# A two-dimensional prefix-sum diagonal: one scan pair for all row groups, another head piece, a finer last load

## The chip, the cores and the metric

The kernel runs on one core of one Trainium2 chip. The metric is device time in microseconds (us) of that core. "The time" is the median of several executions; "the span" is the part of one profiled execution that the hardware profiler covers. All start times below are counted from the start of that span. Engines are named as the profile names them: PE (TensorE), DVE (VectorE), ACT (ScalarE), POOL (GpSimd) and SP (SyncE).

## The reference

The input is four float32 matrices of 4224 x 4224. For each, the two-dimensional prefix sum is taken, its diagonal is read, and the diagonal is summed up once more:

```python
ps = np.cumsum(np.cumsum(x, axis=1), axis=2)
diag = np.diagonal(ps, axis1=1, axis2=2)
return np.cumsum(diag, axis=1).astype(np.float32)
```

Entry i of the diagonal is the sum of the square of rows 0..i and columns 0..i. So it grows, from i-1 to i, by d[i]: the elements of column i above the diagonal, plus the elements of row i up to and with the diagonal. The output is d summed up twice along i. Every element of x is used once, 285.47 MB are read, and only 4 x 4224 numbers are written.

## The kernel before, in words

**Groups.** The rows of one matrix are cut into NG = 11 groups of GW = 384 rows. A group is loaded as one "strip": 128 partitions with 3 neighbouring rows each, all 4224 columns, cast from float32 to bf16 by the transfer. POOL's queue issues these loads (`load_group`, L64). Six strip buffers rotate (NBUF), so a load is issued when the strip six places earlier has been used up.

**What is made of a strip.** For group g the columns fall into three kinds. Columns right of the group lie above the diagonal: PE adds them down over the rows (`columns`, one matmul of 384 columns for each row plane q and each later group j). The selector, a bf16 matrix of zeros with one column of ones, puts the sum into row j of the accumulator d[11, 384] in PSUM. In the group's own 384 columns, `masked` on DVE (L187) multiplies with an upper-triangle mask: the product `mu` goes to PE as the part above the diagonal, and its row sum `ru` is kept. Left of that, whole rows are summed: ACT takes some 9/16 of the columns (`act_sum`, L178), DVE the rest and the group's own columns (`rs`, L297). Row sums minus `ru` give the part at and below the diagonal.

**The end of a matrix.** `sum_up` (L268, L269) forms `rows`; three float32 matmuls with an identity turn them into d. DVE runs two scans over d[11, 384] from zero (L207, L215), PE turns the ends of the groups into the carries of later groups (`carry_ps`, with the small matrices `earlier` and `apart`), and `between` adds `step * carry1 + carry2` to the second scan: the "y step" (L228, L236), on DVE for the first three matrices, on POOL for the last. SP writes y out (L237).

**The last matrix** is arranged so that little is left after the last byte. Its last group (384 rows) is not loaded as a strip. A float32 `head` (the last 128 rows, last 1056 columns) is loaded on SP's queue at the very start. `diag_a`, the 256 x 384 diagonal piece of the other rows, is loaded between strips 0 and 1 of the last matrix and worked on after strip 1. What is left comes behind strip 9: 256 rows in two column pieces (`acuts`), then the last 128 rows in three (`tcuts`). Group 10 has an accumulator of its own, `d_last`, and its own pair of scans `lc`, seeded with `lcarry`. What the late pieces add is summed over rows (`arows` for the 256 rows, `ttot` for the 128) by three helpers at once: PE adds column blocks onto each other with an identity (`fold_in`), ACT sums a second share, DVE a third. Float32 matmuls against weight matrices (`fin_a`, `fin_b`) turn these row sums into what they add to the output, and two adds on DVE (`yl`, L409) and two stores on SP (L410) finish.

The order of the instructions on each engine is written out by hand (`manual_schedule`): an engine runs its instructions in program order.

Of the kernel before, what the change touches and what calls it, by code (L numbers as in the profile page):

```python
# [17 lines left out]
def kernel(  # L18
# [8 lines left out]

    nc = tc.nc

    B, H, W = x.shape  # L30
    N = H
# [4 lines left out]
    LB = B - 1  # L36
    NBUF = 6
# [17 lines left out]
    TB = N - P  # L55
    T0 = N - GW
    HEAD = 1056
    head = last.tile([P, HEAD], FP32, name="head")
    nc.sync.dma_start(out=head, in_=x[LB, TB:N, N - HEAD : N])

# [10 lines left out]

    sel = consts.tile([P, 2 * NG - 1], BF16, name="sel")
    nc.vector.memset(sel, 0.0)
    nc.vector.memset(sel[:, NG - 1 : NG], 1.0)
    ones_col = sel[:, NG - 1 : NG]

    def selector(j):
        return sel[:, NG - 1 - j : 2 * NG - 1 - j]

    def upper_masks(f, w):  # L80
        ums = []
        for q in range(f):
            um = consts.tile([P, w], BF16, name=f"um_{f}_{q}")
            nc.vector.memset(um, 1.0)
            nc.gpsimd.affine_select(  # L85
                out=um,
                in_=um,
                compare_op=ALU.is_gt,
                fill=0.0,
                base=-q,  # L90
                pattern=[[1, w]],
                channel_multiplier=-f,
            )
            ums.append(um)
        return ums

    um3 = upper_masks(F, GW)
# [14 lines left out]
    step_i = consts.tile([NG, GW], I32, name="step_i")  # L112
    nc.gpsimd.iota(step_i, pattern=[[1, GW]], base=1, channel_multiplier=0)
    step = consts.tile([NG, GW], FP32, name="step")
    nc.gpsimd.tensor_copy(out=step, in_=step_i)
# [3 lines left out]
    nc.vector.memset(earlier, 1.0)  # L119
    nc.gpsimd.affine_select(  # L120
        out=earlier,
        in_=earlier,
        compare_op=ALU.is_gt,
        fill=0.0,
        base=0,
        pattern=[[1, NG]],
        channel_multiplier=-1,
    )
    apart_i = consts.tile([NG, NG], I32, name="apart_i")
    nc.gpsimd.iota(apart_i, pattern=[[GW, NG]], base=-GW, channel_multiplier=-GW)  # L130
    apart = consts.tile([NG, NG], FP32, name="apart")
    nc.gpsimd.tensor_copy(out=apart, in_=apart_i)
    nc.gpsimd.affine_select(
        out=apart,
        in_=apart,
        compare_op=ALU.is_gt,
        fill=0.0,
        base=0,
        pattern=[[1, NG]],
        channel_multiplier=-1,  # L140
    )
    um2 = upper_masks(2, GW)
    um1 = upper_masks(1, P)[0]

    def weights(name, q, f, w):

        wi = consts.tile([P, w], I32, name=name + "_i")
        nc.gpsimd.iota(wi, pattern=[[1, w]], base=1 - q, channel_multiplier=-f)
        wt = consts.tile([P, w], FP32, name=name)
        nc.gpsimd.tensor_copy(out=wt, in_=wi)  # L150
        nc.gpsimd.affine_select(
            out=wt,
            in_=wt,
            compare_op=ALU.is_ge,
            fill=0.0,
            base=-q,
            pattern=[[1, w]],
            channel_multiplier=-f,
        )
        return wt  # L160

    w2 = [weights(f"w2_{q}", q, 2, GW) for q in range(2)]
    w1 = weights("w1", 0, 1, P)

# [8 lines left out]
    DUMP = 2176  # L173

    def act_sum(acc, src):
        w = src.shape[-1]
        dump = dumpool.tile([P, DUMP], BF16, name="dump")
        nc.scalar.activation(  # L178
            out=dump[:, :w], in_=src, func=ACT.Copy, accum_out=acc
        )  # L180

    def scalar_cols(g):

        return 0 if g == 0 else (g * GW) * 9 // 16 // 32 * 32
# [11 lines left out]


    NT = 6
    tsum = last.tile([P, NT], FP32, name="tsum")
    hsum = last.tile([P, 2], FP32, name="hsum")  # L200
    hmu = last.tile([P, P], BF16, name="hmu")
    nc.vector.reduce_sum(out=hsum[:, 0:1], in_=head, axis=AX.X)
    masked(hmu, head[:, HEAD - P : HEAD], um1, hsum[:, 1:2])
    nc.vector.tensor_sub(out=tsum[:, 0:1], in0=hsum[:, 0:1], in1=hsum[:, 1:2])

    def scans(d, rows, width, init1, init2, c12):
        nc.vector.tensor_tensor_scan(  # L207
            out=c12[:rows, 0, :width],
            data0=ones_row[:rows, :width],
            data1=d,  # L210
            initial=init1,
            op0=ALU.mult,
            op1=ALU.add,
        )
        nc.vector.tensor_tensor_scan(  # L215
            out=c12[:rows, 1, :width],
            data0=ones_row[:rows, :width],
            data1=c12[:rows, 0, :width],
            initial=init2,
            op0=ALU.mult,  # L220
            op1=ALU.add,
        )

    def between(b, ng, c12, carry_ps, eng):
        carry = smalls.tile([NG, 2], FP32, name="carry")
        nc.vector.tensor_copy(out=carry[:ng, :], in_=carry_ps[:ng, 0:2])  # L226
        y = smalls.tile([NG, GW], FP32, name="y")
        eng.tensor_scalar(  # L228
            out=y[:ng, :],
            in0=step[:ng, :],  # L230
            scalar1=carry[:ng, 0:1],
            scalar2=carry[:ng, 1:2],
            op0=ALU.mult,
            op1=ALU.add,
        )
        eng.tensor_add(out=y[:ng, :], in0=y[:ng, :], in1=c12[:ng, 1, :])  # L236
        nc.sync.dma_start(  # L237
            out=out[b, : ng * GW].rearrange("(g i) -> g i", i=GW), in_=y[:ng, :]
        )

    for b in range(B):
        whole = b < LB
        ng = NG if whole else NG - 1
        d = psum_d.tile([NG, GW], FP32, name="d")
        d_last = None
        if not whole:
            d_last = psum_s.tile([1, GW], FP32, name="d_last")

        first = {"d": True, "l": True}

        def columns(j, lo, hi, rhs):

            if j < ng:
                matmul(d[:, lo:hi], selector(j), rhs, start=first["d"])
                first["d"] = False
            else:
                matmul(d_last[:, lo:hi], ones_col, rhs, start=first["l"])
                first["l"] = False
# [5 lines left out]
        nc.vector.memset(sa[:, 0, :], 0.0)  # L264

        def sum_up(g0, g1):
            gs = slice(g0, g1)
            nc.vector.tensor_add(out=rows[:, gs], in0=rs[:, gs], in1=sa[:, gs])  # L268
            nc.vector.tensor_sub(out=rows[:, gs], in0=rows[:, gs], in1=ru[:, gs])  # L269

        def fold_in(o, src, c0, c1, w):

            for c in range(c0, c1, w):
                matmul(o, ident_h, src[..., c : c + w], start=c == c0)

        for g in range(ng):
            lo, hi = g * GW, (g + 1) * GW
            strip = prefetched.pop((b, g), None)
# [5 lines left out]
            ws = scalar_cols(g)  # L284
            wp = 0
            if not whole and g == ng - 1:

                wp, ws = 1280, 1280 + 1536
                fold9 = psum_s.tile([P, F, 160], FP32, name="fold")
                fold_in(fold9, strip, 0, wp, 160)  # L290
            for q in range(F):
                mu = mup.tile([P, GW], BF16, name="mu")
                masked(mu, strip[:, q, lo:hi], um3[q], ru[:, g, q : q + 1])
                columns(g, 0, GW, mu)
                if ws > 0:
                    act_sum(sa[:, g, q : q + 1], strip[:, q, wp:ws])
            nc.vector.reduce_sum(  # L297
                out=rs[:, g, :], in_=strip[:, :, ws:hi], axis=AX.X
            )
            if not whole and g == 0:  # L300

                diag_a = last.tile([P, 2, GW], BF16, name="diag_a")
                src_a = x[b, T0:TB, :].rearrange("(p f) w -> p f w", f=2)
                nc.gpsimd.dma_start(out=diag_a, in_=src_a[:, :, T0:N])
            if not whole and g == 1:
                NA = 6
                asum = last.tile([P, 2, NA], FP32, name="asum")
                asub = last.tile([P, 2, 2], FP32, name="asub")
                nc.vector.reduce_sum(out=asub[:, :, 0], in_=diag_a, axis=AX.X)
                for q in range(2):  # L310
                    mu = mup.tile([P, GW], BF16, name="mu")
                    masked(mu, diag_a[:, q, :], um2[q], asub[:, q, 1:2])
                    columns(NG - 1, 0, GW, mu)
                columns(NG - 1, GW - P, GW, hmu)
                nc.vector.tensor_sub(
                    out=asum[:, :, 0], in0=asub[:, :, 0], in1=asub[:, :, 1]
                )

        if whole:
            sum_up(0, ng)  # L320
        else:

            strip = strips.tile([P, F, N], BF16, name="strip")
            acuts = [(1536, T0), (0, 1536)]
            for c0, c1 in acuts:
                nc.gpsimd.dma_start(out=strip[:, :2, c0:c1], in_=src_a[:, :, c0:c1])  # L326
# [10 lines left out]
        for q in range(F):  # L337
            matmul(d[:ng, q : GW : F], rows[:, :ng, q], ident)
# [104 lines left out]
```

## Time and profile before

| what | value |
|---|---|
| time, median of 7 runs (lowest to highest) | 671.68 us (671.22 to 673.96) |
| the profiled execution's own time | 671.23 us |
| its span, and what lies around it | 669.5 us, 1.73 us |
| busy PE / DVE / ACT / POOL | 228.3 / 255.9 / 152.9 / 36.5 us |
| software DMA queue | 7440 packets, 142.47 MB written, 99.4% of 16 engines' span |
| mean granted PE clock | 0.648 |

The strips' transfers fill the span; the engines work in bursts of 3 to 8 us after each landing and idle between. Two stretches are not covered by the stream of strips: the first few us, and the work behind the last landings.

### The profile page before, as it was taken

The page shows a single profiled execution, that of the slowest core. Times are in us where ns is not written, and L with a number is a line of the kernel's source. Part 1 is how long each engine was busy: PE and PEld are TensorE (multiplying, and loading weights), DVE is VectorE, ACT ScalarE, POOL GpSimd, SP SyncE. Part 2 cuts the span into 40 slices and gives each one's busy share as a digit, 9 for nine tenths or more (in the row PEclk, how much of TensorE's full clock was granted, in tenths as well). Part 3 has the DMA queues.
Part 4 walks back from the last instruction along what each step waited for, and adds up shares of the span by engine and source line. Part 5 has one row for each costly group of instructions (what it writes and reads, how often), then busy time and mean ns, then how long its engine had stood idle before and what let it go on. Part 6 is the DMA issues. An engine that isn't in the chain of part 4 may idle for free.

```text
span 669.5 us, 2644 instructions
## 1 busy us (share of the span) xinstructions
PE 228.3 (34%) x865; PEld 96.6 (14%) x865; DVE 255.9 (38%) x370; ACT 152.9 (23%) x247; POOL 36.5 (5%) x77
## 2 busy tenths in 40 slices
PE   0454532211155543221125443322213453332225
PEld 0221211000022211100012221110001221111102
DVE  2122333344623333334472222333456222233457
ACT  0011222233301112223330111222342011122344
POOL 6000000000000000000000000000000000000000
PEclk9877676655577776655557676665555676766657
DMA  8999999999999999999999999999999999999995
GB/s 202 218 218 219 218 219 218 217 218 219 218 219 214 215 214 214 217 217 217 219 218 219 218 217 218 217 217 217 218 217 216 217 218 216 215 218 217 218 207 116
DMA packets 7686, 143.23 MB, mean 214 GB/s; under 512 B 845, under 2 KB 1402, under 8 KB 2170
## 3 DMA queue, kind: packets, MB, share of 16 engines
q0 software_dynamic: 7440, 142.47, 99.4%
q1 hardware_dynamic: 234, 0.61, 0.3%
q8 instruction: 6, 0.10, 0.1%
q14 instruction: 6, 0.05, 0.0%
HBM read 285.47 MB, written 0.07 MB: 426 GB/s over the span
## 4 chain that ended last, share of the span: by engine, by line
another core or an unknown queue 53%; DVE 35%; DMA 7%; PE 3%; issue 1%; POOL 0%; DVEq 0%; POOLq 0%
DVE rs L297 23%; DVE mu L187 9%; DMA strip<-in_x_dram 7%; PE d L169 3%; DVE c L215 1%; DVE c L207 1%; PE fin_a L169 0%; DVE lc L215 0%; POOL strip L64 0%; DVE y L236 0%; PE carry_ps L169 0%; PE fin_b L169 0%; DVE lc L207 0%; DVE rows L269 0%
## 5 line engine op out<-in xcount | busy, mean ns | idle before, releaser
L169 PE MATMUL d<-strip,sel 128*11 128x384 bf16 x630 | 174.8, 457 | 354.9 <-DMA strip<-in_x_dram 354.9
L178 ACT ACTIVATE dump<-strip 128x640 bf16<-128x640 bf16 (+12 forms) x123 | 140.2, 1140 | 510.1 <-DMA strip<-in_x_dram 507.6
L187 DVE SCALAR_TENSOR_TENSOR mu<-strip,um 128x384 bf16<-128x384 bf16 x129 | 65.2, 555 | 394.8 <-DMA strip<-in_x_dram 394.8
L297 DVE TENSOR_REDUCE rs<-strip 128x3 f32<-128x1152 bf16 (+11 forms) x43 | 167.1, 3886 | 0.0
L169 PEld LDWEIGHTS <-sel 128*11 128x11 bf16 (+1 forms) x792 | 90.1, 114 | 527.8 <-issue 505.7
L64 POOL DMA_DIRECT2D strip<-in_x_dram x43 | 23.0, 537 | 534.7 <-PE d L169 281.6
L169 PE MATMUL d<-mu,sel 128*11 128x384 bf16 x129 | 37.4, 399 | 40.5 <-DVE mu L187 40.5
L178 ACT ACTIVATION_READ_ACCUMULATOR dump<-strip 128x1 f32 x123 | 22.9, 186 | 0.0
L169 PE MATMUL d_last<-strip,sel 128*1 128x384 bf16 x30 | 9.0, 424 | 11.9 <-DMA strip<-in_x_dram 11.9
L169 PE MATMUL d<-ident,rows 128*11 128x128 f32 (+1 forms) x24 | 5.2, 379 | 21.4 <-DVE rows L269 21.4
L187 DVE DVE_READ_ACCUMULATOR mu<-strip,um 128x1 f32 x129 | 10.7, 83 | 0.0
L169 PEld LDWEIGHTS d<-ident,rows 128*11 128x11 f32 (+1 forms) x24 | 2.5, 118 | 25.4 <-DVE rows L269 16.9
L207 DVE TENSOR_TENSOR_SCAN c<-ones_row,d 11x384 f32<-11x384 f32 (+1 forms) x4 | 3.8, 942 | 4.8 <-PE d L169 4.7
L169 PE MATMUL fold<-strip,ident_h 128*128 128x480 bf16 (+1 forms) x13 | 4.5, 524 | 1.5 <-DMA strip<-in_x_dram 1.5
L215 DVE TENSOR_TENSOR_SCAN c<-ones_row,c 11x384 f32<-11x384 f32 (+1 forms) x4 | 3.8, 945 | 0.1
L228 POOL TENSOR_SCALAR y<-step,carry 10x384 f32<-10x384 f32 x1 | 0.7, 651 | 54.2 <-DVE carry L226 54.2
L169 PE MATMUL carry_ps<-c,earlier 11*11 11x2 f32 (+2 forms) x10 | 0.8, 159 | 7.7 <-DVE c L215 7.7
L330 POOL DMA_DIRECT2D strip<-in_x_dram x3 | 1.6, 537 | 22.1 <-PE d L169 14.2
L169 PEld LDWEIGHTS <-ident_h 128*128 128x128 bf16 x19 | 2.1, 124 | 4.7 <-issue 4.1
L85 POOL TENSOR_SCALAR_AFFINE_SELECT um<-um 128x384 bf16<-128x384 bf16 (+1 forms) x6 | 2.7, 480 | 0.1
L326 POOL DMA_DIRECT2D strip<-in_x_dram x2 | 1.4, 709 | 13.4 <-PE d L169 13.4
L169 PE MATMUL fin_a<-w,arows 128*1 128x256 f32 x4 | 2.1, 634 | 0.0
(64 smaller groups left out, 37.5 us busy)
## 6 DMA issues: line engine op xcount, KB each, us to landing
strip<-in_x_dram POOLq DMA_DIRECT2D x43, 3168.0 KB, 82.9
strip<-in_x_dram POOLq DMA_DIRECT2D x1, 1152.0 KB, 74.7
strip<-in_x_dram POOLq DMA_DIRECT2D x1, 768.0 KB, 77.6
strip<-in_x_dram POOLq DMA_DIRECT2D x1, 568.0 KB, 65.5
head<-in_x_dram SPq DMA_DIRECT2D x1, 528.0 KB, 3.6
diag_a<-in_x_dram POOLq DMA_DIRECT2D x1, 192.0 KB, 84.0
strip<-in_x_dram POOLq DMA_DIRECT2D x1, 160.0 KB, 65.8
strip<-in_x_dram POOLq DMA_DIRECT2D x1, 64.0 KB, 57.6
```

The source lines that it names most:

```text
L64: nc.gpsimd.dma_start(out=t, in_=x[b, r0 : r0 + GW, :].rearrange("(p f) w -> p f w", f=F))
L85: nc.gpsimd.affine_select(out=um, in_=um, compare_op=ALU.is_gt, fill=0.0, base=-q, pattern=[[1, w]], channel_multiplier=-f,)
L169: nc.tensor.matmul(o, lhsT=lhsT, rhs=rhs, start=start, stop=False, skip_group_check=True)
L178: nc.scalar.activation(out=dump[:, :w], in_=src, func=ACT.Copy, accum_out=acc)
L187: nc.vector.scalar_tensor_tensor(out=o, in0=i, scalar=1.0, in1=m, op0=ALU.mult, op1=ALU.mult, accum_out=acc,)
L207: nc.vector.tensor_tensor_scan(out=c12[:rows, 0, :width], data0=ones_row[:rows, :width], data1=d, initial=init1, op0=ALU.mult, op1=ALU.add,)
L215: nc.vector.tensor_tensor_scan(out=c12[:rows, 1, :width], data0=ones_row[:rows, :width], data1=c12[:rows, 0, :width], initial=init2, op0=A ...
L228: eng.tensor_scalar(out=y[:ng, :], in0=step[:ng, :], scalar1=carry[:ng, 0:1], scalar2=carry[:ng, 1:2], op0=ALU.mult, op1=ALU.add,)
L297: nc.vector.reduce_sum(out=rs[:, g, :], in_=strip[:, :, ws:hi], axis=AX.X)
L326: nc.gpsimd.dma_start(out=strip[:, :2, c0:c1], in_=src_a[:, :, c0:c1])
L330: nc.gpsimd.dma_start(out=tail[:, 0, c0:c1], in_=x[b, TB:N, c0:c1])
```

## The change

- **One accumulator and one scan pair for all 11 groups.** Row k = (j + 1) mod 11 of d holds group j, so that group 10 is row 0 and the ten others are rows 1 to 10. `d_last`, `lc`, `lcarry` and the scans for them go.
- **Scans seeded by weighted totals.** DVE first sums each row of d (`pu` column 0), and sums d times 384, 383, ..., 1 (`to_end`; `pu` column 1). PE makes the carries of these sums, and the scans start from the carries. The y step goes; SP writes the second scan out, in two stores for a whole matrix.
- **The head piece** is now the 256 rows' last 528 columns (rows h * 128 + p instead of 2p + h), masked once for each half at the start. The piece of the last 128 rows that comes between the strips, `diag_b`, is 128 x 128.
- **The late pieces.** The 256 rows come in columns 1536 to 3696 and 0 to 1536; the last 128 rows in four pieces of 1664, 1408, 704 and 320 columns.
- The row sums of strip 9 of the last matrix go through `parts` and one reduction over it; the sums of strips 0 to 8 are formed before strip 9 is worked on.

```diff
-    head = last.tile([P, HEAD], FP32, name="head")
-    nc.sync.dma_start(out=head, in_=x[LB, TB:N, N - HEAD : N])
+    HC = 528
+    src_a = x[LB, T0:TB, :].rearrange("(h p) w -> p h w", p=P)
+    head = last.tile([P, 2, HC], FP32, name="head")
+    nc.sync.dma_start(out=head, in_=src_a[:, :, N - HC : N])
...
+    def row_of(j):
+        return (j + 1) % NG
...
+    to_end = counted("to_end", NG, GW, [(0, GW, GW, -1, 0)])
...
             if not whole and g == 0:
-                diag_a = last.tile([P, 2, GW], BF16, name="diag_a")
-                nc.gpsimd.dma_start(out=diag_a, in_=src_a[:, :, T0:N])
+                diag_b = last.tile([P, P], BF16, name="diag_b")
+                nc.gpsimd.dma_start(out=diag_b, in_=x[b, TB:N, TB:N])
...
-            sum_up(0, ng - 1)
-            nc.vector.reduce_sum(out=f9, in_=fold9, axis=AX.X)
-            nc.vector.tensor_add(out=rs[:, ng - 1], in0=rs[:, ng - 1], in1=f9)
-            sum_up(ng - 1, ng)
+            nc.vector.tensor_scalar_mul(
+                out=parts[:, :, 2], in0=ru[:, k, :], scalar1=-1.0
+            )
+            row_sums(parts[:, :, 3], fold_g)
+            row_sums(rows[:, k, :], parts)
...
-            acuts = [(1536, T0), (0, 1536)]
+            acuts = [(1536, N - HC), (0, 1536)]
...
-            tcuts = [(896, N - HEAD), (256, 896), (0, 256)]
+            bcuts = [(2432, TB), (1024, 2432), (320, 1024), (0, 320)]
...
-        scans(d[:ng, :], ng, GW, 0.0, 0.0, c12)
-        matmul(carry_ps[:ng, 0:2], earlier[:ng, :ng], c12[:ng, :, GW - 1], start=True)
-        matmul(carry_ps[:ng, 1:2], apart[:ng, :ng], c12[:ng, 0, GW - 1 : GW])
-        if whole:
-            between(b, ng, c12, carry_ps, nc.vector)
-            continue
-        nc.vector.tensor_copy(out=lcarry, in_=lcarry_ps)
-        between(b, ng, c12, carry_ps, nc.gpsimd)
-        scans(d_last, 1, GW, lcarry[:, 0:1], lcarry[:, 1:2], lc)
+        row_sums(pu[:, 0:1], d)
+        masked(c12[:, 1, :], d, to_end, pu[:, 1:2])
+        matmul(carry_ps, earlier, pu, start=True)
+        matmul(carry_ps[:, 1:2], apart, pu[:, 0:1])
+        nc.vector.tensor_copy(out=carry, in_=carry_ps)
+        for i, src in enumerate((d, c12[:, 0, :])):
+            nc.vector.tensor_tensor_scan(
+                out=c12[:, i, :], data0=ones_row, data1=src,
+                initial=carry[:, i : i + 1], op0=ALU.mult, op1=ALU.add,
+            )
+        nc.sync.dma_start(
+            out=out[b, :T0].rearrange("(g i) -> g i", i=GW), in_=c12[1:NG, 1, :]
+        )
+        if whole:
+            nc.sync.dma_start(out=out[b, T0:N].unsqueeze(0), in_=c12[0:1, 1, :])
+            continue
...
+        shares = [(768, 512), (512, 512), (256, 224)]
+        n = 1
+        for i, ((c0, c1), (wp, wa)) in enumerate(zip(bcuts, shares)):
+            fold_in(fold_b, part_b[:, 0], c0, c0 + wp, 256, start=i == 0)
+            act_sum(tsum[:, n : n + 1], part_b[:, 0, c0 + wp : c0 + wp + wa])
+            row_sums(tsum[:, n + 1 : n + 2], part_b[:, 0, c0 + wp + wa : c1])
+            n += 2
+            if i == 0:
+                matmul(fin_b, arows[:, 0:1], weights[:, 2 * P : GW], start=True)
+                matmul(fin_b, arows[:, 1:2], weights[:, P : 2 * P])
+                matmul(fin_a, arows[:, 0:1], weights[:, 0 : 2 * P], start=True)
+                matmul(fin_a[:, P : 2 * P], arows[:, 1:2], weights[:, 0:P])
+        row_sums(tsum[:, n : n + 1], fold_b)
+        c0, c1 = bcuts[3]
+        row_sums(tsum[:, n + 1 : n + 2], part_b[:, 0, c0:c1])
```

The second share of the 256 rows, columns 0 to 1536, is split between PE (768) and ACT (768) only; before, DVE had 128 of them. The final adds take group 10 from row 0 of the scan instead of `lc`.

## The prediction

> **What bounds the kernel now.** I read the page's busy shares and queues first, to see which resource fills the span; then the chain of waits near the end; then the timeline around the last landings.
>
> ```profile
> PE 228.3 (34%) x865; PEld 96.6 (14%) x865; DVE 255.9 (38%) x370; ACT 152.9 (23%) x247; POOL 36.5 (5%) x77
> ...
> DMA  8999999999999999999999999999999999999995
> ...
> q0 software_dynamic: 7440, 142.47, 99.4%
> ```
>
> No engine is busy over 38%, the software queue 99.4%. In the packet records the strips land every 14.96 us, and last bytes land at 663.16. So an edit to work that lies between landings is worth nothing; what counts is the time of the last bytes and what follows them. The windows show where the stream ends (columns: stretch, its length, busy PE, PEld, DVE, ACT, POOL, clock, DMA share, GB/s):
>
> ```profile
> 662.00:663.00 1.00, 0.92 (x5) 0.56 (x4) 1.00 (x3) 0.88 (x1) 0.00 (x0) 0.50 0.42 64
> 663.00:664.00 1.00, 0.30 (x2) 0.00 (x0) 0.90 (x4) 0.80 (x4) 0.00 (x0) 0.50 0.00 0
> ```
>
> The span ends at 669.5, so 6.3 us lie behind the bytes. The chain of waits says who fills them (start, length, what):
>
> ```profile
> 656.59 0.84 PE d L169 x6
> ...
> 658.43 0.96 DVE c L215
> ...
> 660.11 0.98 DVE lc L207
> 661.11 1.63 DVE lc L215
> 662.74 0.31 DVE asum L378
> 663.05 0.61 DVE asum L381
> ...
> 663.76 0.18 DVE arows L383
> ...
> 664.07 0.59 PE fin_b L169 x2
> 664.65 0.85 PE fin_a L169 x2
> 665.51 0.43 PE fin_b L169 x2
> 665.93 0.87 PE fin_a L169 x2
> ...
> 667.25 0.28 DVE yl L409
> ```
>
> It does not run through the last landing. DVE does two scan pairs, the second (`lc`, 2.6 us) holds up the sums of the 256 rows, so `arows` comes at 663.93, and PE needs 2.6 us for four float32 products. `ttot` had been ready since 665.24. The last add ends at 667.53; 1.97 us of store and closing follow, which I keep. The profiled execution took 671.23, 1.73 over its span and 0.45 under the median; I take the gain from it and subtract that from the median.
>
> **Landings.** `diag_a` delays strip 1 of the last matrix: DVE begins on strips 0 and 1 as follows, 16.16 apart instead of 14.96.
>
> ```profile
> 514.32 0.56 DVE L187 SCALAR_TENSOR_TENSOR mu<-strip,um 128x384 bf16<-128x384 bf16 x1 [1.14 <-DMA strip<-in_x_dram]
> ...
> 530.48 0.56 DVE L187 SCALAR_TENSOR_TENSOR mu<-strip,um 128x384 bf16<-128x384 bf16 x1 [13.37 <-DMA strip<-in_x_dram]
> ```
>
> Landings themselves are 16.12 apart, so it costs 1.16 us. It has 256 packets of 768 B written at 79 ns, 16 on each engine. `diag_b` has 128 of 256 B, 8 on each. No data packet here is that small; the bounds are the 4-byte semaphore packet (22 ns) and the 512 B packet (60 ns), so 0.18 to 0.48 us. A line through 60 ns at 512 B and 79 ns at 768 B gives 41 ns, 0.33 us, which I take. The head becomes 256 packets of 2112 B instead of 128 of 4224 B at 164 ns; with the 1536 B output packets of that queue at 78 ns a line gives 96 ns, so 16 x 96 - 8 x 164 = 0.22 us more; but its packets run from 2.1 to 4.3 us while the strips' begin at 3.7, so part is hidden: 0 to 0.22, I take 0.08. Strip 9 lands 1.16 - 0.33 - 0.08 = 0.75 earlier, and DVE begins on it at 649.45 instead of 650.20.
>
> [...]
>
> The late pieces move the same bytes. From the records (361 ns at 4608 B, 248 at 3072, 356 at 4544, 116 at 1280, 60 at 512) and the line between them, an engine's packets took 16 x (361 + 248) + 8 x (356 + 116 + 60) = 14.0 us and will take 16 x (340 + 248) + 8 x (267 + 229 + 126 + 69) = 14.9; with the diagonal pieces it is 15.3 both times. So the last bytes still land at about 663.2; the landings measured 0.95 of such sums (5.50 of 5.78 for the first piece). After 649.35 I get 654.5 and 658.2 for the two pieces of 256 rows, 660.3, 661.95, 662.9 and 663.3 for the four others.
>
> **Strip 9 to d.** Masks and the sum of 3072 columns stay: 650.20 to 654.91, when DVE took its next instruction, so 654.16 now. Before, six instructions followed until 656.53; now the two sums over 27 columns are done ahead of the strip, and `parts` takes 0.10 + 0.65 + 0.11 + 0.17: `rows` at 655.19. The six matmul passes (0.84 at full clock) end at 656.09. At the ends of earlier matrices they took 1.45 at half clock, so 0 to 0.6 more.
>
> **d to arows.** Gone: the pair `lc`, 0.98 + 1.63. Gone from POOL: the y step, which ran beside the slow scan; that scan has the shape of the others at 0.95. Added ahead of the scans: a sum and a masked sum of d from PSUM. The profile has neither on 11 x 384 float32 in PSUM; nearest are `y` (0.55 for 11 x 384 float32) and `fold` (0.65 for 480 in PSUM). I take 0.55 and 0.56; ends are 0.4 (256 columns in PSUM) and twice the value. They end at 657.23 with the accumulator's 0.08. PE's carry: 0.14 of issue, 0.25 for four passes; copy 0.15; scans 1.00 (the price with a seed from memory) and 0.95, up to 1.63 each: done at 659.72. Behind these waits on DVE stand all sums of the late pieces, ACT and PE going on meanwhile: PE's second fold into `fold_a` is done at 659.1, ACT's two shares of 768 columns at 660.25 (0.97 apart, by 0.86 for 640 and the slope between its rows). Then DVE's 0.67 for `fold_a` and 0.17: `arows` at 660.63, 3.3 us earlier, and PE may start at 660.77.
>
> **The last pieces.** PE first folds the piece that landed at 660.3, three blocks until 660.9. The four products hold 5 blocks of 128 columns, 0.42 each (2.51 us for 6 before, start to start, at half clock), and end at 663.0. Behind them stand three more folds, 0.25 each and 0.15 to drain: 663.95. That is later than the last landing, so finer pieces buy nothing themselves. DVE: 0.33 to the next start, 0.47 for 320 columns, 0.11 and 0.16 for `ttot`: 665.05. Then 0.14, PE 0.64, 0.03, the last add 0.28: 666.14. The first add no longer waits for PE. Against 667.53 the gain is 1.39 us: 0.75 from order of bytes, 0.64 from the chain.
>
> **Edits at nothing.** Ends of the first three matrices: y's 0.47 and 0.55 go, 0.55 and 0.64 come; the chain there ended 1.04 us before the next strip, and each strip is issued some 83 us before it lands, so even 10 us late would cost nothing. SP's extra store per matrix queues ahead of nothing but the next matrix's. Masks of the head are done before the first strip at 19.3. `diag_b` work stands after strip 1, where DVE idles 7 us. POOL's last piece waits for strip 7, some 40 us before its turn, nothing behind it. Wider selectors for group 10 cost 33 ns a matmul in idle time.
>
> **Rivals.** *Full clock for the products.* The granted clock fell to 0.5 at 661.42; if the stretch at 1.0 lasts, products and folds take half of 2.1 + 0.75: 668.9. For it: the clock changes by steps of 3.4 us that a run need not repeat. Against: the time before would share it. *Gain eaten.* Rows at half clock (+0.6), `diag_b` and head at their ends (+0.3), less 0.13 of slack before the products: 671.05. For it: 1.45 at three of four matrix ends. *Slower: DVE's line in front of `fold_a`.* From d to the second scan I have 3.63 us. Everything beyond 0.13 more goes to the end. With both sums doubled (+1.1), both scans at 1.63 (+1.3) and rows at half clock (+0.6), the time is 673.2; it is slower than before from 5.2 us on. For it: sums and scans on 11 partitions, one waiting on another, are all on the path now. Against: the slow scan stood alone beside POOL.
>
> **How the numbers follow.** 671.68 - 1.39 = 670.3. This kernel's measurement can tell some 0.2%, 1.34 us, from no change, and the forecast lies just past it: of its chance of 0.52, 0.32 is faster and 0.20 within. Full clock 0.20 (faster), gain eaten 0.17 (within), slower 0.11. So faster 0.52, same 0.37, slower 0.11. The range is 668.9 to 672.2: the slower case and the far half of full clock are left out.
>
> **What would show it.** Strip 9 at 649.4, one scan pair with its second scan under 1 us, `arows` before 661, PE's products starting behind the fold at 660.9, `ttot` as the last thing waited for, last landing near 663.2. I am wrong if `arows` is still what PE waits for after 661.5, if the bytes end later than 663.5, or if a scan or sum over d takes over 1.2 us.

## The result, and the profile after

The changed kernel takes 669.80 us (median of 18 runs, 669.18 to 671.01) against 671.96 us (44 runs, 671.19 to 674.13) for the kernel before. The ratio is 0.9967, 95% interval 0.9961 to 0.9974: 2.2 us less, where 1.4 were forecast. The profiled execution took 670.09 us, its span is 667.6 instead of 669.5. What lies around the span was 2.5 us in this execution and 1.7 before, so profiles are compared by their spans and times by their medians.

The stream of strips is as full as before (page, queues):

```profile
q0 software_dynamic: 7456, 142.47, 99.7%
```

The windows around the last bytes (same columns as before) show them at nearly the same place: the last piece has landed at 663.50, 0.34 later than before. The clock column now reads 1.00 where it read 0.50.

```profile
662.00:663.00 1.00, 0.70 (x5) 0.29 (x4) 0.55 (x1) 0.71 (x2) 0.00 (x0) 1.00 0.34 52
663.00:664.00 1.00, 0.27 (x1) 0.00 (x0) 0.90 (x3) 0.49 (x3) 0.00 (x0) 1.00 0.02 3
```

DVE begins on strip 9 0.45 us earlier than in the kernel before (first the line of before, then the line of after):

```profile
650.20 0.56 DVE L187 SCALAR_TENSOR_TENSOR mu<-strip,um 128x384 bf16<-128x384 bf16 x1 [7.98 <-DMA strip<-in_x_dram]
```

```profile
649.75 0.56 DVE L195 SCALAR_TENSOR_TENSOR mu<-strip,um 128x384 bf16<-128x384 bf16 x1 [7.47 <-DMA strip<-in_x_dram]
```

The chain of waits of the changed kernel, from d to the last add:

```profile
655.50 0.95 PE d L175 x6
...
656.95 0.55 DVE c L195 x2
...
658.09 1.01 DVE c L329
...
659.12 1.01 DVE c L329
660.13 0.59 DVE asum L192
...
660.82 0.16 DVE arows L192
660.98 0.46 DVE tsum L192
661.44 0.77 another core or an unknown queue
...
662.23 0.55 DVE tsum L192
662.78 0.29 another core or an unknown queue
...
663.10 1.15 DVE tsum L192 x3
...
664.35 0.17 DVE ttot L192
...
664.56 0.39 PE fin_b L175 x2
...
664.98 0.28 DVE yl L378
```

One scan pair instead of two; `arows` at 660.98 instead of 663.93; and then the chain leaves PE. The two entries of "an unknown queue" are waits for the pieces of the last 128 rows. After the last of them come three sums, `ttot`, one product, one add. PE's own timeline says why its four products are no longer in the chain (start, length, operation, idle time before and what ended it):

```profile
661.13 0.60 PE L175 MATMUL fin_b<-weights,arows 128*1 128x128 f32 x4
661.56 0.81 PE L175 MATMUL fin_a<-weights,arows 128*1 128x256 f32 x4
662.31 0.39 PE L175 MATMUL fold<-strip,ident_h 128*128 128x256 bf16 x2
663.12 0.27 PE L175 MATMUL fold<-strip,ident_h 128*128 128x256 bf16 x1 [0.42 <-DMA strip<-in_x_dram]
```

From the first product to the next fold it is 1.18 us, at full clock, where the kernel before, at half clock (0.50 in the windows from 662 to 666) and with six blocks of 128 columns instead of five, needed 2.51 from its first to its fifth; PE then waits for bytes.

### The profile page after: what moved, and what is told of

Read it like the earlier page. It is cut to its first block, busy times and chain, and to the rows that moved or that the text cites. A ratio compares the mean times of both kernels' runs of the same rounds, so it can differ in the third digit from the quotient of the medians.

```text
span 667.6 us, 2641 instructions
## 1 busy us (share of the span) xinstructions
PE 227.2 (34%) x862; PEld 95.7 (14%) x862; DVE 253.5 (38%) x371; ACT 153.3 (23%) x249; POOL 33.0 (5%) x72
## 4 chain that ended last, share of the span: by engine, by line
another core or an unknown queue 54%; DVE 36%; DMA 7%; PE 1%; issue 1%; POOL 0%; DVEq 0%; POOLq 0%
DVE rs L192 24%; DVE mu L195 9%; DMA strip<-in_x_dram 7%; DVE c L329 1%; PE d L175 1%; DVE parts L192 1%; DVE tsum L192 0%; DVE c L195 0%; POOL strip L70 0%; DVE pu L192 0%; PE carry_ps L175 0%; DVE rows L242 0%; DVE rows L243 0%; DVEq L195 0%
## 5 line engine op out<-in xcount | busy, mean ns | idle before, releaser
L175 PE MATMUL d<-strip,sel 128*11 128x384 bf16 x660 | 182.5, 456 | 369.3 <-DMA strip<-in_x_dram 369.3
L187 ACT ACTIVATE dump<-strip 128x192 bf16<-128x192 bf16 (+13 forms) x124 | 140.5, 1133 | 509.5 <-DMA strip<-in_x_dram 506.7
L175 PEld LDWEIGHTS <-sel 128*11 128x11 bf16 x792 | 89.8, 113 | 530.6 <-issue 508.5
L192 DVE TENSOR_REDUCE rs<-strip 128x3 f32<-128x1152 bf16 (+10 forms) x42 | 163.7, 3898 | 0.0
L175 PE MATMUL d<-ident,rows 128*11 128x128 f32 x24 | 5.3, 384 | 20.3 <-DVE rows L243 19.9
L175 PEld LDWEIGHTS d<-ident,rows 128*11 128x11 f32 x24 | 2.6, 119 | 24.5 <-DVE rows L243 15.0
L192 DVE TENSOR_REDUCE pu<-d 11x1 f32<-11x384 f32 x4 | 2.2, 546 | 5.2 <-PE d L175 5.2
L329 DVE TENSOR_TENSOR_SCAN c<-ones_row,carry,c 11x384 f32<-11x384 f32 x4 | 4.0, 1005 | 0.1
L329 DVE TENSOR_TENSOR_SCAN c<-ones_row,carry,d 11x384 f32<-11x384 f32 x4 | 4.0, 1000 | 0.1
L192 DVE TENSOR_REDUCE parts<-strip 128x3 f32<-128x3072 bf16 x1 | 3.3, 3347 | 0.0
```

Source lines behind the costliest of these rows:

```text
L175: nc.tensor.matmul(o, lhsT=lhsT, rhs=rhs, start=start, stop=False, skip_group_check=True)
L187: nc.scalar.activation(out=dump[:, :w], in_=src, func=ACT.Copy, accum_out=acc)
L192: nc.vector.reduce_sum(out=acc, in_=src, axis=AX.X)
L329: nc.vector.tensor_tensor_scan(out=c12[:, i, :], data0=ones_row, data1=src, initial=carry[:, i : i + 1], op0=ALU.mult, op1=ALU.add,)
```

## The experiments

After the result I had two theories. The first: the end now hangs on the last bytes, and much of the line of scans is hidden. The second, as forecast: the line of DVE and PE work sets the end, and each part of the change takes its share out of it. Every ratio is against the kernel before on the same chip (medians 671.56 to 671.82 there), with its 95% interval; the changed kernel gave 669.80, 669.86 and 669.83 on three occasions.

**The second scan pair put back** (two_pairs).

```diff
+        lc = last.tile([1, 2, GW], FP32, name="lc")
+        for i, src in enumerate((d[0:1, :], lc[:, 0, :])):
+            nc.vector.tensor_tensor_scan(
+                out=lc[:, i, :], data0=ones_row[0:1, :], data1=src,
+                initial=carry[0:1, i : i + 1], op0=ALU.mult, op1=ALU.add,
+            )
...
-                out=yl[:, c0:c1], in0=fin, in1=c12[0:1, 1, c0:c1]
+                out=yl[:, c0:c1], in0=fin, in1=lc[:, 1, c0:c1]
```

> The changed kernel with the second scan pair put back: two scans of 1 x 384 for group 10 behind the common pair, some 2.0 us more on DVE ahead of the sum of fold_a; the final adds read them. Theory of the last bytes: in the changed kernel PE and DVE wait for the last pieces, and about 0.7 us of the scans' line is hidden while the products run at full clock; the time is 1.0 to 1.4 us over the changed kernel's 669.8, ratio to before 0.9983 to 0.9989. Rival, the chain as it was forecast (0.13 us of slack): 1.9 us over it, ratio 0.9995 to 0.9997. Second rival, the scans are hidden altogether and the gain comes from the order of the bytes: unchanged, ratio 0.9967.

Measured: 671.99 us, ratio 1.0003 (0.9994 to 1.0012). All of the gain is gone, 2.2 us for 2.0 us of scans. The chain shows two prices:

```profile
660.39 0.92 DVE lc L346
661.31 0.02 issue
661.33 1.00 DVE lc L346
...
663.33 1.01 PE fin_b L175 x4
664.34 1.28 PE fin_a L175 x4
665.62 0.77 PE fold L175 x3
```

`arows` comes 2.2 us later (0.36 of it because this execution began later on strip 9), and the products, which now start after PE has idled 1.94 us, take 2.29 us instead of 1.18: the clock had fallen to half at 663.13 (it read 0.56 from 663 to 664). My theory of the last bytes falls, and so does the rival that the scans were hidden. The chain as it was forecast, 1.9 us over the changed kernel, is nearest, but it had the products at half clock in both kernels.

**The transfers of before under the new scans** (old_stream): head of 128 rows, `diag_a`, late pieces in two and three parts.

```diff
-    head = last.tile([P, 2, HC], FP32, name="head")
-    nc.sync.dma_start(out=head, in_=src_a[:, :, N - HC : N])
+    head = last.tile([P, HEAD], FP32, name="head")
+    nc.sync.dma_start(out=head, in_=x[LB, TB:N, N - HEAD : N])
...
-            bcuts = [(2432, TB), (1024, 2432), (320, 1024), (0, 320)]
+            bcuts = [(896, N - HEAD), (256, 896), (0, 256)]
...
-        shares = [(768, 512), (512, 512), (256, 224)]
+        shares = [(1280, 992), (0, 320)]
```

> The changed kernel with the transfers of before: head of 128 rows x 1056 columns, diag_a of 256 x 384 between the strips, late pieces in two and three parts. Theory of the last bytes: strip 9 begins 0.4 to 0.5 us later again but the line of scans has room, and the last bytes land 0.2 to 0.3 us earlier, so the time is within 0.3 us of the changed kernel's 669.8 where the products get full clock, and up to 0.9 over it where they do not; ratio 0.9965 to 0.9980. Rival, the gain is half the order of the bytes, as forecast (0.75 of 1.39): 0.7 to 1.1 us over the changed kernel, ratio 0.9977 to 0.9984, at any clock.

Measured: 670.58 us, ratio 0.9978 (0.9969 to 0.9987), 0.8 us over the changed kernel. The number fits the rival, and as well the theory's case of products at half clock. The chain shows the way:

```profile
662.04 1.23 PE fold L175 x5
663.26 0.94 PE fin_b L175 x4
664.21 1.29 PE fin_a L175 x4
```

The 2272-column piece lands at 662.00 and stands before the products in PE's order. The products wait for it and not for `arows`, which ended at 661.42, and take 2.24 us, beside 2.29 in *two_pairs* at half clock and 1.18 in the changed kernel at full. So what counts is the landing of the first piece of the last rows; how much of that is its size, and how much the later turn of strip 9, this run does not separate.

**Coarse pieces** (coarse): the changed kernel with the first two pieces of the last 128 rows in one.

```diff
-            bcuts = [(2432, TB), (1024, 2432), (320, 1024), (0, 320)]
+            bcuts = [(1024, TB), (320, 1024), (0, 320)]
...
-        shares = [(768, 512), (512, 512), (256, 224)]
+        shares = [(1280, 896), (256, 224)]
```

> The changed kernel with the last 128 rows in three pieces: the first two (1664 and 1408 columns) are one of 3072, with 5 fold blocks on PE, 896 columns on ACT and 896 on DVE. Theory that the piece sizes matter because the first piece stands before the products in PE's order: it lands at 662.2 instead of 660.5, the products start at 662.9 or later instead of 661.1, and the time is 0.6 us (full clock) to 2.0 us (half clock) over the changed kernel's 669.8. Rival, as forecast, that finer pieces buy nothing themselves: within 0.2 us of it.

Measured: 671.82 us, ratio 1.0003 (0.9994 to 1.0012). The finer pieces alone are worth as much as the whole change, against my forecast that they buy nothing. PE's timeline:

```profile
661.87 1.23 PE L175 MATMUL fold<-strip,ident_h 128*128 128x256 bf16 x5 [2.85 <-DMA strip<-in_x_dram]
663.02 1.01 PE L175 MATMUL fin_b<-weights,arows 128*1 128x128 f32 x4
663.83 1.48 PE L175 MATMUL fin_a<-weights,arows 128*1 128x256 f32 x4
665.25 0.39 PE L175 MATMUL fold<-strip,ident_h 128*128 128x256 bf16 x1
```

PE idles 2.85 us for the large piece, does fold and products at half clock (it read 0.50 from 662 to 666), and the last small fold and DVE's sum of it stand behind the products. From the start of the large fold to the end of the last add it is 5.84 us; in *old_stream*, with the same five blocks, products at half clock too, but no fold behind them, it is 4.19.

**Is it the clock?** Three kernels get matmuls that nobody reads, in the stretch where PE idles: *coarse* 18 (coarse_warm), *two_pairs* 14 (two_pairs_warm), the kernel before 10 ahead of the fold of the last rows and 6 behind it (warm_before). The edit of coarse_warm:

```diff
+                for _ in range(18):
+                    matmul(
+                        fin_a, sel[:, NG - 1 : NG], part_a[:, 0, 0:256], start=True
+                    )
                 fold_in(fold_b, part_b[:, 0], c0, c0 + wp, 256, start=i == 0)
```

> The kernel of the run coarse with 18 matmuls of 256 columns that nobody reads, on PE ahead of the fold of the 3072-column piece, where PE had idled 2.85 us. Theory that the clock makes most of what the coarse pieces cost: fold, products and last product run at full clock, the last add ends 1.5 to 1.9 us earlier, time 670.1 to 670.5 (ratio 0.9975 to 0.9982). Rival, the later start of the products (by the landing of the larger piece) makes it and the clock little: 0 to 0.6 us lower than coarse, 671.2 to 671.8.

> The kernel of the run two_pairs with 14 matmuls of 256 columns that nobody reads, on PE between the fold of the first piece and the products, where PE had idled 1.94 us. Theory: of the 2.2 us that the second scan pair costs, 1.0 to 1.4 come from the half clock of the products and folds behind it; time 670.6 to 671.0 (ratio 0.9982 to 0.9988). Rival, the pair costs its own 2 us on DVE and nothing by the clock: 671.8 to 672.0.

> The kernel before with 16 matmuls of 256 columns added on PE in the last stretch, 10 ahead of the first fold of the last 128 rows and 6 behind that fold, into the bank of fin_a before fin_a is begun: work that nobody reads. Theory that the clock fell at 661.4 because PE had idled before the products: they now run at full clock, 1.2 instead of 2.5 us, and the time falls by 0.9 to 1.2 us to 670.4 to 670.8 (ratio 0.9983 to 0.9987). Rival, the clock's steps come by the phase of the execution: products at half clock as often as before, time unchanged (ratio 1.0000) or a little over.

Measured: coarse_warm 670.24 us, ratio 0.9977 (0.9968 to 0.9987), 1.6 us under *coarse*. two_pairs_warm 670.95 us, 0.9987 (0.9977 to 0.9997), 1.0 under *two_pairs*. warm_before 670.66 us, 0.9989 (0.9979 to 0.9998), 0.9 under the kernel before. All three lie where the theory of the clock had put them: work that computes nothing makes them faster. The intervals of *coarse* and coarse_warm lie apart, those of *two_pairs* and two_pairs_warm just touch, and that of warm_before ends just under 1. The windows (stretch, length, busy PE, clock, DMA share, GB/s), of *coarse* first, then of coarse_warm:

```profile
660.00:662.00 2.00, 0.13 (x1) 0.57 0.93 166
```

```profile
660.00:662.00 2.00, 1.23 (x12) 1.00 0.96 177
```

So by the medians, of the 2.0 us by which *coarse* is slower than the changed kernel, 1.6 go with the clock, and 0.4 are left for the later start. From the large fold to the last add it is now 3.97 us instead of 5.84. In the profile of two_pairs_warm the added matmuls began only at 660.84, and the 14 of them took 3.06 us where the 18 of coarse_warm took 2.13 at full clock. They held the products up until 663.70, where `arows` had ended at 662.72; the runs of this kernel spread from 670.25 to 672.64.

**The slow scan of the kernel before** (before_no_y): the y step of the last matrix left out.

```diff
-        between(b, ng, c12, carry_ps, nc.gpsimd)
+        nc.sync.dma_start(
+            out=out[b, : ng * GW].rearrange("(g i) -> g i", i=GW),
+            in_=c12[:ng, 1, :],
+        )
```

> The kernel before, with the y step of the last matrix left out: the second scan is stored as it is, so the first 10 groups of the fourth matrix lack their carries. Theory that the slow scan of 1.63 us was held up by POOL's y step: it takes 0.95 to 1.05 us, arows comes 0.6 us earlier, and the time falls by 0.6 us (ratio 0.9990). Rival, one partition or the seed makes that scan slow: it stays at 1.6 us and the time too.

Measured: 670.92 us, ratio 0.9990 (0.9981 to 0.9999). The scan takes 1.00 us, on the same single partition and with the same seed:

```profile
661.90 1.00 DVE L215 TENSOR_TENSOR_SCAN lc<-ones_row,lcarry,lc 1x384 f32<-1x384 f32 x1
```

In the kernel before, POOL's adds lay beside it:

```profile
660.95 0.98 POOL L236 TENSOR_TENSOR y<-y,c 10x384 f32<-10x384 f32 x1
```

**The price of `diag_b`** (no_diag_b; one run).

```diff
-                nc.gpsimd.dma_start(out=diag_b, in_=x[b, TB:N, TB:N])
+                nc.vector.memset(diag_b, 0.0)
```

> The changed kernel without the load of diag_b (128 x 128 elements, set to zero instead and so left out of the sums). If its packets alone make up the 0.73 us by which strip 1 of the last matrix landed later than its turn, the gap between the landings of strips 0 and 1 falls from 15.69 to 14.96; if they cost 0.33, as forecast, and the rest is an instruction load at 514 us on the same engine, it falls to 15.3 to 15.4.

Measured: by the ends of their last packets, strips 0 and 1 of the last matrix land 15.27 us apart instead of 15.69; 669.06 us. That pair alone would give the piece 0.42, and 0.31 to something else. But the same gap is 14.96 to 15.69 in the nine profiles that load `diag_b`, with a median of 15.38, and 15.27 lies among them. So one execution does not settle the price. An instruction load of some 320 ns lies near that stretch in every profile (at 513.77 here, at 513.98 in the changed kernel); what it adds was not separated.

**A version without late folds** (no_late_folds, no_late_folds_2): the second and third piece are summed by ACT and DVE alone, so that nothing stands behind the products.

```diff
-        shares = [(768, 512), (512, 512), (256, 224)]
+        shares = [(768, 512), (0, 704), (0, 352)]
...
-            fold_in(fold_b, part_b[:, 0], c0, c0 + wp, 256, start=i == 0)
+            if i == 0:
+                fold_in(fold_b, part_b[:, 0], c0, c0 + wp, 256, start=True)
...
                 matmul(fin_a[:, P : 2 * P], arows[:, 1:2], weights[:, 0:P])
-        row_sums(tsum[:, n : n + 1], fold_b)
+                row_sums(tsum[:, n : n + 1], fold_b)
+                n += 1
```

> The changed kernel without the folds of the second and third piece of the last 128 rows on PE: ACT takes 704 and 352 columns, DVE 704 and 352, and the sum of fold_b is taken early, between the first and second piece. Chain theory: the products no longer hold up anything but the last product, so the time is 0.1 us lower where they run at full clock and 0.6 to 0.8 lower at half clock; median 669.2 to 669.6. Rival, the time hangs on DVE's sums after the last bytes at any clock: unchanged, 669.8.

> The kernel of the run no_late_folds once more, beside the changed kernel on the same chip. If the folds behind the products cost time only at half clock, its median is 0.1 to 0.5 us under the changed kernel's and its slowest runs are cut: 669.3 to 669.7 against 669.8. If it was chance: the same.

> The changed kernel once more, on the same chip as the next three. The chain theory (the scans' line and PE's products set the end; bytes only where the products get full clock): time 669.6 to 670.0, ratio 0.9965 to 0.9970; products 1.2 us long at full clock or 2.2 at half, and the span 667.4 to 668.6 accordingly.

> The changed kernel, for the comparison with no_late_folds_2: 669.7 to 669.9, with single runs up to 671 where the products fall into a stretch at half clock.

Measured: 669.15 and 669.20 us, ratios 0.9961 (0.9949 to 0.9974) and 0.9960 (0.9948 to 0.9972), beside 669.86 and 669.83 for the changed kernel, 0.9972 (0.9961 to 0.9984) and 0.9966 (0.9955 to 0.9977). The ratios' intervals overlap, but on both occasions the median is 0.6 to 0.7 us lower, a little more than expected, and its ten runs lie at 668.72 to 669.57, where the changed kernel's 33 lie at 669.00 to 671.02. The two profiles show why it holds. In the first the products took as long as in the changed kernel at full clock:

```profile
660.90 0.60 PE L175 MATMUL fin_b<-weights,arows 128*1 128x128 f32 x4
661.34 0.81 PE L175 MATMUL fin_a<-weights,arows 128*1 128x256 f32 x4
```

In the second they fell into half clock (it read 0.50 from 660 to 662), and it cost nothing.

```profile
661.37 1.01 PE L175 MATMUL fin_b<-weights,arows 128*1 128x128 f32 x4
662.17 1.39 PE L175 MATMUL fin_a<-weights,arows 128*1 128x256 f32 x4
664.44 0.38 PE L175 MATMUL fin_b<-weights,ttot 128*1 128x128 f32 x2 [0.87 <-DVE ttot L192]
```

PE is done with them 0.87 us before the product of `ttot`, and the last add ends at 665.14 with the last bytes at 663.6. From DVE's start on strip 9 to the end of the last add it is 15.28 us in both profiles; the changed kernel's three profiles, all with products of the same length (0.60 and 0.81 us) at full clock, have 15.51 to 15.53. So some 0.25 us is gained at full clock too; no profile caught the changed kernel at half clock, to show the rest. It is the fastest of the versions that sum up everything.

## Why the prediction was right or wrong

The direction held, and the mechanism in the main: the kernel before ended with 4.4 us of DVE and PE work behind the last landing, and one scan pair in place of two took `arows` off the late path (*two_pairs*). What the end then waited for was forecast wrongly, and so was the clock of the products. The size lay between the forecast and its first rival, and that it lay so near is in part luck: the chain gained 1.18 us more than forecast, and the start of strip 9 and the closing took 0.67 of that back. Step by step:

- **Landings.** Strip 9 was forecast 0.75 earlier; DVE began on it at 649.75, 0.45 earlier. That is one pair of executions. With the old transfers DVE began on strip 9 at 650.16 to 650.37 (four profiles), with `diag_b` at 649.42 to 650.36 (nine, median 649.64), which makes 0.6 by the medians. The term for the piece between the strips held: the gap between strips 0 and 1 is 16.12 to 16.39 with `diag_a`, its median with `diag_b` is 15.38, and the medians differ by 0.87 where 1.16 - 0.33 = 0.83 was forecast. The packets of `diag_b` took 41 ns, as the line gave. The head's packets took 86 ns, not 96; its 0.08 can't be seen, since the first strip landed at 19.31 to 20.19 with the old head and at 19.54 to 20.36 with the new one.
- **Strip 9 to d.** `rows` ended 5.70 us after DVE's start, forecast 5.74; the matmul passes took 0.93, forecast 0.84, since full clock came only at 655.76.
- **d to arows.** 3.70 us from d to the second scan, forecast 3.63: sum 0.55, masked sum 0.53, scans 1.00 and 1.01. The rival of a slow DVE line is out, and before_no_y shows that the slow scan had been held up beside POOL.
- **The last pieces.** Two steps failed here. "Finer pieces buy nothing themselves" is wrong by 2.0 us (*coarse*): I had looked at the last landing alone, and not at what a larger first piece makes PE wait for. And the products were priced at half clock because the profile before had them so. They took 1.18 us, and the last add ended at 665.26 instead of 666.14. I had named full clock a rival and put it down to chance of phase. The added matmuls show that it hangs also on how busy PE is ahead of them: from 660 to 662 *coarse* had 0.13 us of matmuls and a clock of 0.57, coarse_warm 1.23 us and 1.00, and in warm_before the four products took 1.31 us, start to start, instead of 2.51. That the change itself made full clock likelier is my estimate from these. Chance of phase is a part of it all the same: *no_late_folds* and *no_late_folds_2* are one kernel, and its products took 1.25 us in one profile and 2.20 in the other. In the kernel before the clock fell at 661.12; the prediction's 661.42 is 0.30 late, and no sum rests on it. My own mark for the last bytes, 663.5, was just reached: 663.50.
- **The closing.** I kept 1.97 us behind the last add; it was 2.34. The three profiles with the old stores (the kernel before, before_no_y, warm_before) have 2.0 to 2.1, all others 2.3 to 2.4. The last store's packet begins 0.7 us after the add in both; the rest lies behind it. The changed kernel issues three more stores; whether these make it was not tried.

At the last add the profiles differ by 667.53 - 665.26 = 2.27 us, 0.45 of it from strip 9's start and 1.82 from the chain; 0.37 of it is lost in the closing, which leaves the 1.9 of the spans. The parts do not add up: taking back the scan pair alone, or the finer pieces alone, costs the whole gain, because in either case PE idles, 1.94 us before the products or 2.85 us before the fold that stands ahead of them, and does the products at half clock. The clock alone is worth 0.9 us in the kernel before (warm_before).

## What to carry to other kernels

Behind a full DMA stream, price each landing by what stands behind it in an engine's order, not by the last byte alone: a large piece in front of a chain of products delays them all (the 3072-column piece of *coarse*: 2.0 us, half clock included). Price TensorE work at the end of a kernel with the idle time ahead of it, since waits of 1.94 us (*two_pairs*) and 2.85 us (*coarse*) were paid twice here, once as a wait and once as half clock (products of 2.29 and 2.23 us instead of 1.18); and take folds that other engines can do out from behind the products (0.6 to 0.7 us in *no_late_folds*). Before a gap between two landings is taken as the price of one transfer, look at the same gap in several executions: here it ran from 14.96 to 15.69 us for the same transfers.

## What the runs showed of the hardware

In the profile of the kernel before, the granted clock read 1.00 from 654.29 to 661.12 and 0.50 from there to the last add. In the changed kernel's it read 1.00 from 655.76 past the last add. In the last 3.41 us before its fall the kernel before had 1.55 us of matmuls (657.71 to 661.12); the changed kernel had 2.11 us in the 3.41 us from 659.17 to 662.58, and its clock stayed. (3.41 us is the shortest stretch at one clock in both of these profiles, as from 623.57 to 626.99 in the kernel before.) *coarse* fell at 660.30 (its clock read 0.65 from 660 to 661), with 1.04 us of matmuls in the 3.41 us before, so PE had not been idle all that time. Matmul ends are modelled in the profile, so these busy times are good to some hundredths. What makes the clock fall or rise, and at which busy share, was not shown.

A scan on DVE of 1 x 384 float32 with both inputs in SBUF took 1.63 us beside POOL's elementwise work (the kernel before) and 1.00 without it (before_no_y).
